# A running sum in PSUM for the seven products of Winograd's form

## The chip, the core and the metric

The kernel runs on one core of a Trainium2 chip. The metric is device time: microseconds (us) from the start of the program to its end on that core. The engines are named as the profile names them: PE multiplies matrices (PEld is its loading of weights), DVE does element-wise work on tensors, ACT does activation functions, casts and copies, POOL does further element-wise work, SP issues transfers. Each engine takes its own instructions in order; semaphores tell one engine that another is done. PE writes its sums into PSUM, a memory of eight banks; a product of 128 x 512 f32 fills one bank.

## What is computed

One layer of a backbone over 1024 latent tokens of width 1024, with a context of 256 tokens. Two token mixers (retention and mLSTM) are lifted to full width, gated and added, and a SwiGLU feed-forward follows. What the change touches are two of its projections:

```python
def mixer_output(ret, ml, rg, mo, bg_ret, bg_ml, w_ret_up, w_ml_up, w_out):
    ...
    merged = jax.nn.sigmoid(bg_ret) * (y_ret @ w_ret_up) + jax.nn.sigmoid(bg_ml) * (y_ml @ w_ml_up)
    return merged @ w_out

def swiglu(h, w_ffn_in, w_ffn_out):
    gate, up = jnp.split(h @ w_ffn_in, 2, axis=-1)
    return (jax.nn.silu(gate) * up) @ w_ffn_out
```

`bg_ret` and `bg_ml` are two groups of columns of one input projection, 1024 inputs to 1024 outputs each; `w_ffn_in` has 1024 inputs and 2 x 2816 outputs.

## The kernel before

**Precision.** Every operand is kept as two f32r parts, hi + lo. `split` (L173, L174) makes them: ACT casts the value to hi, DVE subtracts hi from it to give lo. A product is three matmuls: hi with hi, hi with lo, lo with hi.

**Blocks.** The two projections above are done in blocks of 256 outputs by 1024 inputs by 1024 tokens. Cut into halves in each dimension, a block is a 2 x 2 by 2 x 2 product of matrices, and Winograd's form of Strassen's method does it with seven products in place of eight. `seven` loads the four raw tiles of a block's weights (`raw_quads`, tiles `raw`, four buffers) and yields the seven left factors: four of them sums and differences that DVE makes (L209, tiles `stg`, three buffers), s1 to s4, and the raw a11, a12, a22. `w_pairs` splits them in the order in which they are yielded, two to a buffer (tiles `whi` and `wlo`, four buffers each). The right factors b11 to b22 and t1 to t4 are made once for all blocks of a stage.

`prod` (L228 to L231) is one product of 512 inputs, 128 outputs and 512 tokens: four steps of three matmuls each, 12 matmuls of 128 x 512 into one bank. A block is 84 matmuls.

`winograd_block` before takes seven PSUM banks, one for each product, in the order a11, a12, s2, s3, s1, s4, a22. ACT copies the first product to SBUF (L267, p1). Everything else is added by DVE, which reads a bank and a tile in SBUF (L255): u2 = second factor's product + p1, u3, u4, and the four results (0,0), (1,1), (0,1), (1,0) = (half of the outputs, half of the tokens). `ps` is one of two pools of four banks each, `mm` and `sc`; blocks take the one and the other in turn (L931, L1056), and a bank is taken again when its reader is done. The sums go to tiles `cp`, the results to tiles `sg` or `hid`, of four buffers each.

**The two stages.** In the gate stage (L908 to L931) seven blocks are done, the first of branch 1, then branch 0 and branch 1 in turn. For each of a block's four results `bg_done` follows: ACT's Sigmoid (L920), POOL's product with the lifted branch (L921), and for branch 1 DVE's sum with the result of branch 0 (L925) and a store. The first of those blocks has its partners from earlier; its tags are `hid`, those of branch 0 are `sg`. The output projection (L93 to L95) comes next and begins with the merged tiles. In the first FFN projection (L1045 to L1056) there are 20 blocks, gate and up in turn: ACT's Silu for the one (`gate_done`, L991, tiles `sg`), POOL's product and a store for the other (`up_done`, L995, L996, tiles `hid`). While a block is computed the next one's weights are loaded, added and split by `seven`.

**What sets the order.** Nothing is placed by hand: a tile scheduler puts each engine's instructions in a fixed order when the program is built, and tiles come free when their last reader is done. So the order in which ACT, DVE and PE do things around a block follows from the code's order and from the scheduler.

Of the kernel before, what the change touches and what calls it, by code (L numbers as in the profile page):

```python
# [15 lines left out]
ALU = mybir.AluOpType  # L16

P = 128
D = 1024
# [5 lines left out]
EPS = 1e-6  # L25
# [11 lines left out]
def body(tc, a, out):  # L37
# [33 lines left out]

    # ---------------------------------------------------------------- weights
    def load_w_half(src, kn, cn, hf):
# [11 lines left out]
    def load_w(src, kn, cn):  # L85
        """Loads the two halves of a block and splits each into f32r parts hi + lo."""
        return [load_w_half(src, kn, cn, hf) for hf in range(2)]

    def mm3(ps, pairs):
        """ps = sum over pairs ((lhi, llo), (rhi, rlo)) of (lhi + llo)^T (rhi + rlo)."""  # L90
        n = len(pairs)
        for i, ((lh, ll), (rh, rl)) in enumerate(pairs):
            nc.tensor.matmul(ps, lhsT=lh, rhs=rh, start=i == 0, stop=False)  # L93
            nc.tensor.matmul(ps, lhsT=lh, rhs=rl, start=False, stop=False)  # L94
            nc.tensor.matmul(ps, lhsT=ll, rhs=rh, start=False, stop=i == n - 1)  # L95

    # -------------------------------------------------------------- constants
    cpack = const.tile([P, 218], F32, name="cpack")
# [16 lines left out]
    def rsqrt_small(v, y, t):  # L115
        """y = v ** -0.5 by an integer seed and Newton steps."""
        nc.vector.tensor_scalar(out=t.bitcast(I32), in0=v.bitcast(I32), scalar1=1, scalar2=None,
                                op0=ALU.logical_shift_right)
        nc.vector.tensor_scalar(out=y.bitcast(I32), in0=t.bitcast(I32), scalar1=-1.0,
                                scalar2=float(0x5F3759DF), op0=ALU.mult, op1=ALU.add)  # L120
        for _ in range(3):
            nc.vector.tensor_tensor(out=t, in0=y, in1=y, op=ALU.mult)
            nc.vector.scalar_tensor_tensor(out=t, in0=t, scalar=-0.5, in1=v, op0=ALU.mult, op1=ALU.mult)
            nc.vector.scalar_tensor_tensor(out=y, in0=t, scalar=1.5, in1=y, op0=ALU.add, op1=ALU.mult)

    def rms_cols(parts, n):
        """(sum of squares / D + EPS) ** -0.5 of each token, as columns."""
        nb = n // P
        pc = sc_ps()[:, :nb]
        for b in range(nb):  # L130
            for i, x in enumerate(parts):
                nc.tensor.matmul(pc[:, b:b + 1], lhsT=x[:, b * P:(b + 1) * P], rhs=ones[:, 0:1],
                                 start=i == 0, stop=i == len(parts) - 1)
        v, y, t = (const.tile([P, 4], F32, tag="rms", bufs=6, name=nm("rms"))[:, :nb] for _ in range(3))
        nc.vector.tensor_scalar(out=v, in0=pc, scalar1=1.0 / D, scalar2=EPS, op0=ALU.mult, op1=ALU.add)
        rsqrt_small(v, y, t)
        dg = stage()[:, :n]
        nc.vector.tensor_tensor(out=dg.rearrange("p (b t) -> p b t", b=nb), in0=ident.unsqueeze(1).to_broadcast([P, nb, P]),
                                in1=y.unsqueeze(2).to_broadcast([P, nb, P]), op=ALU.mult)
        return dg  # L140

    def rms_bcast(dg):
        """PSUM: the columns as rows, on all partitions."""
        pr = sc_ps()[:, :dg.shape[1]]
        nc.tensor.matmul(pr, lhsT=ones, rhs=dg, start=True, stop=True)
        return pr
# [4 lines left out]
    def log_sigmoid(pl, o, x, shape, key):  # L151
        """o = min(x, 0) - log1p(exp(-|x|)), log1p by the series of 2 atanh(e / (2 + e))."""
        def t(s):
# [14 lines left out]

    # ------------------------------------------------------ Winograd's form
    tmps = []  # L170
# [20 lines left out]
    def w_pairs(blocks):  # L191
        """f32r parts hi + lo of the blocks, two to a buffer."""
        res = []
# [9 lines left out]
    def seven(src):  # L203
        """The seven left factors of Winograd's form, from the four blocks of 512 inputs x 128 columns."""
        r = raw_quads(src)

        def tt(x, y, op):
            o = stage()
            nc.vector.tensor_tensor(out=o, in0=x, in1=y, op=op)  # L209
            return o  # L210

        def gen():
            s1 = tt(r["a21"], r["a22"], ALU.add)
            yield r["a11"]
            s2 = tt(s1, r["a11"], ALU.subtract)
            yield r["a12"]
            yield s2
            yield tt(r["a11"], r["a21"], ALU.subtract)
            yield s1
            yield tt(r["a12"], s2, ALU.subtract)  # L220
            yield r["a22"]

        return w_pairs(gen())

    def prod(ps, w, x, start, stop):
        """ps (+)= w^T x over 512 inputs."""
        for k in range(4):
            c = slice(k * P, (k + 1) * P)  # L228
            nc.tensor.matmul(ps, lhsT=w[0][:, c], rhs=x[0][:, k, :], start=start and k == 0, stop=False)  # L229
            nc.tensor.matmul(ps, lhsT=w[0][:, c], rhs=x[1][:, k, :], start=False, stop=False)  # L230
            nc.tensor.matmul(ps, lhsT=w[1][:, c], rhs=x[0][:, k, :], start=False, stop=stop and k == 3)  # L231

# [16 lines left out]
    def winograd_block(ps, w, x, t, done, tag):  # L249
        a11, a12, s2, s3, s1, s4, a22 = w  # L250
        b11, b21, b12, b22 = x
        t1, t2, t3, t4 = t

        def add(p, v, o):
            nc.vector.tensor_tensor(out=o, in0=p, in1=v, op=ALU.add)  # L255
            return o

        def put(f, hf, p, v):
            done(f, hf, add(p, v, tmp(tag)))

        def product(w_, x_):
            p = ps()
            prod(p, w_, x_, True, True)
            return p

        p1, u2, u3, u4 = (tmp("cp") for _ in range(4))
        nc.scalar.copy(p1, product(a11, b11))  # L267
        put(0, 0, product(a12, b21), p1)
        add(product(s2, t2), p1, u2)
        add(product(s3, t3), u2, u3)  # L270
        p5 = product(s1, t1)
        add(p5, u2, u4)
        put(1, 1, p5, u3)
        put(0, 1, product(s4, b22), u4)
        put(1, 0, product(a22, t4), u3)

    # ------------------------------------------------- modulation and first norm
    es_ctx = ExitStack()
# [69 lines left out]
    def first_tiles(kts):  # L348
        """The first projection's products with feature tiles kts, for the first four chunks of latents."""
        for n in (2, 3, 4, 5):  # L350
# [9 lines left out]
    def tok(n, kt):  # L360
        """f32r parts of the modulated tokens of chunk n, feature tile kt."""
        if n < 2:
# [118 lines left out]
    def scan(u):  # L481
        """The two directions of a head, as stages at slots: a generator that emits a slot at a time."""
        k, v, q, g = bufs[u]
# [218 lines left out]
    def ada2():  # L702
        """Modulation columns 16 ..: two tiles of 128 at a time."""
        for cb in range(16):
# [101 lines left out]

    # ------------------------------------------------------- lift and merge
    def up_mm(br, w, y, c, dt_, hf):
# [50 lines left out]
    def diff(o, x, k, y):  # L859
        """o = x - y of feature tile k, x as f32r parts and y whole or as parts."""  # L860
        hi, lo = (v[:, k, :].bitcast(F32) for v in x)
# [79 lines left out]

    # -------------------------------------------- output projection, second norm
    x1_d = dram.tile([2, KT, P, 512], F32, name="x1_d")
# [36 lines left out]

    # --------------------------------------------------------------------- ffn
    pe = pool(es, "pe", side="right")
# [15 lines left out]
    def right_factors(k):  # L998
        """Feature tiles k of the sums and differences of the token blocks; the last stays in xf."""
        x12, x22 = xf[1][:, k, :], xf[1][:, 4 + k, :]  # L1000
# [56 lines left out]

    # ------------------------------------------------- ffn output, final norm
    es_pt.close()
# [11 lines left out]
    def w2_tiles(dp, extra=None):  # L1071
        """Weights of 256 outputs for hidden tiles 0 .. 21, as f32r parts, in order of the tiles."""
        for b in range(11):
# [14 lines left out]
    def hidden(hf):  # L1088
        """Loads and splits the hidden tiles of a half of the tokens, one at a time in order."""
        big = None  # L1090
# [112 lines left out]
def _layout(x, c, ctx, c_ctx, w_ada, b_ada, norm1_gain, norm2_gain, w_in, mlstm_gate_bias, ret_decay_logit,  # L1203
# [4 lines left out]
    def kblock(w):  # L1208
        """[K, C] -> [2, 128, K / 256, C] with row k = (2 half, K / 256, 128)."""
        k, n = w.shape  # L1210
        return w.reshape(2, k // 256, P, n).transpose(0, 2, 1, 3)
# [57 lines left out]
```

## Time and profile before

| | |
|---|---|
| median of three runs | 1644.67 us |
| lowest and highest run | 1643.19 and 1646.52 us |
| profiled execution, span of the core | 1643.1 us |
| instructions | 25962 |
| PE busy | 1604.8 us, 98% of the span |
| DVE, ACT, POOL busy | 1005.4, 631.2, 423.6 us |

The profile gives one execution's span and no other time of it; the three runs are others. Busy time is read as time in which an engine ran at least one instruction. A line such as `731.45 0.19 PEld L231 ... [0.54 <-DVE wlo L174]` of a timeline is an instruction's start in the span, its duration, engine, line, operation, what it writes and reads, and in brackets how long the engine was idle before it and whose result ended that.

### The profile page before, as it was taken

The page shows a single profiled execution, that of the slowest core. Times are in us where ns is not written, and L with a number is a line of the kernel's source. Part 1 is how long each engine was busy: PE and PEld are TensorE (multiplying, and loading weights), DVE is VectorE, ACT ScalarE, POOL GpSimd, SP SyncE. Part 2 cuts the span into 40 slices and gives each one's busy share as a digit, 9 for nine tenths or more (in the row PEclk, how much of TensorE's full clock was granted, in tenths as well). Part 3 has the DMA queues.
Part 4 walks back from the last instruction along what each step waited for, and adds up shares of the span by engine and source line. Part 5 has one row for each costly group of instructions (what it writes and reads, how often), then busy time and mean ns, then how long its engine had stood idle before and what let it go on. Part 6 is the DMA issues. An engine that isn't in the chain of part 4 may idle for free.

```text
span 1643.1 us, 25962 instructions
## 1 busy us (share of the span) xinstructions
PE 1604.8 (98%) x9326; PEld 1395.8 (85%) x9326; DVE 1005.4 (61%) x2223; ACT 631.2 (38%) x1512; POOL 423.6 (26%) x593
## 2 busy tenths in 40 slices
PE   7998999999999999999999999999999999999997
PEld 2798999999999998888877777888888888887887
DVE  5768555644645445678875777667677666536233
ACT  4555332333435355443343453323333334423230
POOL 1546244332322422233330225111111111001001
PEclk9999999999999999999999999999999999999998
DMA  9211223332432244444457412222222224735531
GB/s 328 103 62 35 73 84 104 100 101 91 136 104 91 71 149 135 161 173 161 142 183 252 130 56 71 90 96 85 96 84 83 92 88 168 268 108 179 162 103 52
DMA packets 114033, 199.13 MB, mean 121 GB/s; under 512 B 13104, under 2 KB 24048, under 8 KB 113904
## 3 DMA queue, kind: packets, MB, share of 16 engines
q1 hardware_dynamic: 112032, 195.38, 36.1%
q10 hardware_dynamic: 1872, 2.10, 0.4%
q8 instruction: 73, 1.20, 0.3%
q14 instruction: 56, 0.46, 0.1%
HBM read 160.66 MB, written 36.77 MB: 120 GB/s over the span
## 4 chain that ended last, share of the span: by engine, by line
PE 79%; DVE 7%; POOL 5%; issue 5%; DMA 2%; ACT 1%; SPq 0%; DVEq 0%; POOLq 0%; ACTq 0%
PE mm L95 9%; PE mm L93 9%; PE mm L94 9%; PE mm L1127 5%; PE mm L1129 5%; PE sc L229 5%; PE sc L230 5%; PE sc L231 5%; PE mm L1128 5%; PE mm L229 5%; PE mm L231 5%; PE mm L230 5%; PE sc L511 2%; PE sc L328 1%; POOL hid L995 1%
## 5 line engine op out<-in xcount | busy, mean ns | idle before, releaser
L93 PE MATMUL mm<-whi,A 128*128 128x256 f32 (+1 forms) x992 | 289.8, 292 | 0.9 <-DVE gtok L468 0.9
L95 PE MATMUL mm<-whi,A 128*128 128x256 f32 (+1 forms) x992 | 281.7, 284 | 0.2 <-DVE A L316 0.2
L94 PE MATMUL mm<-wlo,A 128*128 128x256 f32 (+1 forms) x992 | 281.3, 284 | 0.0
L174 DVE TENSOR_TENSOR wlo<-raw,whi 128x512 fp32r<-128x512 f32 x178 | 132.1, 762 | 114.8 <-ACT whi L173 114.6
L93 PEld LDWEIGHTS mm<-whi,A 128*128 128x128 f32 x992 | 190.3, 192 | 1.4 <-DVE gtok L468 1.1
L173 ACT CAST whi<-raw 128x512 fp32r<-128x512 f32 x178 | 106.2, 619 | 221.6 <-PE mm L1128 79.8
L95 PEld LDWEIGHTS mm<-whi,A 128*128 128x128 f32 x992 | 190.2, 192 | 0.5 <-DVE A L316 0.4
L94 PEld LDWEIGHTS mm<-wlo,A 128*128 128x128 f32 x992 | 190.6, 192 | 0.0
L995 POOL TENSOR_TENSOR hid<-hid,sg 128x512 f32<-128x512 f32 x44 | 84.8, 1931 | 329.0 <-DVE hid L255 294.0
L229 PE MATMUL mm<-A,whi 128*128 128x512 f32 x320 | 124.7, 390 | 2.4 <-DVE sg L255 1.7
L230 PE MATMUL mm<-A,whi 128*128 128x512 f32 x320 | 125.2, 391 | 1.0 <-DVE A L316 1.0
L231 PE MATMUL mm<-A,wlo 128*128 128x512 f32 x320 | 125.0, 391 | 0.0
L82 DVE TENSOR_TENSOR wlo<-raw,whi 128x512 fp32r<-128x512 f32 (+1 forms) x112 | 76.4, 708 | 53.6 <-ACT whi L81 53.6
L173 ACT CAST whi<-stg 128x512 fp32r<-128x512 f32 x108 | 61.9, 618 | 106.7 <-PE sc L230 62.2
L81 ACT CAST whi<-raw 128x512 fp32r<-128x512 f32 (+1 forms) x112 | 65.3, 619 | 41.1 <-PE mm L94 13.9
L497 POOL TENSOR_SCALAR vs<-v,colq 128x129 f32<-128x129 f32 x72 | 48.0, 676 | 127.6 <-PE sc L511 127.6
L229 PE MATMUL sc<-A,whi 128*128 128x512 f32 x208 | 80.9, 389 | 0.0
L230 PE MATMUL sc<-A,whi 128*128 128x512 f32 x208 | 80.9, 389 | 0.0
L231 PE MATMUL sc<-A,wlo 128*128 128x512 f32 x208 | 80.9, 389 | 0.0
L174 DVE TENSOR_TENSOR wlo<-stg,whi 128x512 fp32r<-128x512 f32 x108 | 80.0, 779 | 0.7 <-ACT whi L173 0.7
L1127 PE MATMUL mm<-A,whi 128*128 128x512 f32 (+1 forms) x204 | 77.8, 382 | 0.0
L1129 PE MATMUL mm<-A,wlo 128*128 128x512 f32 (+1 forms) x204 | 77.8, 381 | 0.0
(350 smaller groups left out, 4057.1 us busy)
## 6 DMA issues: line engine op xcount, KB each, us to landing
raw<-wffn SPq DMA_DIRECT2D x88, 256.0 KB
raw<-wfo SPq DMA_DIRECT2D x88, 256.0 KB
raw<-wada SPq DMA_DIRECT2D x64, 256.0 KB
raw<-win SPq DMA_DIRECT2D x60, 256.0 KB
hid_d<-hid SPq DMA_DIRECT2D x44, 256.0 KB
hraw<-hid_d SPq DMA_DIRECT2D x40, 256.0 KB
araw<-wada SPq DMA_DIRECT2D x32, 256.0 KB
bc<-rows_d SPq DMA_DIRECT2D x64, 128.0 KB
```

Of the source, the lines that this page charges most:

```text
L93: nc.tensor.matmul(ps, lhsT=lh, rhs=rh, start=i == 0, stop=False)
L94: nc.tensor.matmul(ps, lhsT=lh, rhs=rl, start=False, stop=False)
L95: nc.tensor.matmul(ps, lhsT=ll, rhs=rh, start=False, stop=i == n - 1)
L173: nc.scalar.copy(hi, x)
L174: nc.vector.tensor_tensor(out=lo, in0=x, in1=hi.bitcast(F32), op=ALU.subtract)
L229: nc.tensor.matmul(ps, lhsT=w[0][:, c], rhs=x[0][:, k, :], start=start and k == 0, stop=False)
L230: nc.tensor.matmul(ps, lhsT=w[0][:, c], rhs=x[1][:, k, :], start=False, stop=False)
L231: nc.tensor.matmul(ps, lhsT=w[1][:, c], rhs=x[0][:, k, :], start=False, stop=stop and k == 3)
L995: nc.gpsimd.tensor_tensor(out=c, in0=c, in1=sgs[f, hf], op=ALU.mult)
L1127: nc.tensor.matmul(ps, lhsT=w[0][:, c], rhs=h[0][:, t], start=kt == 0, stop=False)
L1128: nc.tensor.matmul(ps, lhsT=w[0][:, c], rhs=h[1][:, t], start=False, stop=False)
L1129: nc.tensor.matmul(ps, lhsT=w[1][:, c], rhs=h[0][:, t], start=False, stop=kt == 2 * NG - 1)
```

## The change

The seven left factors come in another order: a11, s1, s2, a12, s3, s4, a22. A block takes three banks in place of seven. In the first, `chain`, four products are added up one after the other: a11 b11, then s2 t2, s3 t3 and a22 t4, without clearing the bank between. After each of the first three ACT copies the sum so far to a tile `cp`; these are p1, u2 and u3 of before, and after the fourth ACT copies the bank as the result (1,0). The second bank takes a12 b21, and DVE adds p1 to give (0,0). The third takes s1 t1; DVE adds u3 to give (1,1); then s4 b22 is added to the same bank, and DVE adds u2 to give (0,1). So a block has three additions of DVE for seven, and four copies of ACT for one. The three matmuls a step stand in one line now (L230), and those of the added products carry the stop flag each.

```diff
         def gen():
+            yield r["a11"]
             s1 = tt(r["a21"], r["a22"], ALU.add)
-            yield r["a11"]
+            yield s1
             s2 = tt(s1, r["a11"], ALU.subtract)
+            yield s2
             yield r["a12"]
-            yield s2
             yield tt(r["a11"], r["a21"], ALU.subtract)
-            yield s1
             yield tt(r["a12"], s2, ALU.subtract)
             yield r["a22"]
...
-    def prod(ps, w, x, start, stop):
-        """ps (+)= w^T x over 512 inputs."""
+    def prod(ps, w, x, start, stop, cont=False):
         for k in range(4):
             c = slice(k * P, (k + 1) * P)
-            nc.tensor.matmul(ps, lhsT=w[0][:, c], rhs=x[0][:, k, :], start=start and k == 0, stop=False)
-            nc.tensor.matmul(ps, lhsT=w[0][:, c], rhs=x[1][:, k, :], start=False, stop=False)
-            nc.tensor.matmul(ps, lhsT=w[1][:, c], rhs=x[0][:, k, :], start=False, stop=stop and k == 3)
+            for i, (wp_, xp) in enumerate(((0, 0), (0, 1), (1, 0))):
+                nc.tensor.matmul(ps, lhsT=w[wp_][:, c], rhs=x[xp][:, k, :], start=start and k == i == 0,
+                                 stop=cont or (stop and k == 3 and i == 2), skip_group_check=cont)
...
     def winograd_block(ps, w, x, t, done, tag):
-        a11, a12, s2, s3, s1, s4, a22 = w
+        a11, s1, s2, a12, s3, s4, a22 = w
         b11, b21, b12, b22 = x
         t1, t2, t3, t4 = t
-        def add(p, v, o):
-            nc.vector.tensor_tensor(out=o, in0=p, in1=v, op=ALU.add)
+        def put(f, hf, p, v):
+            c = tmp(tag)
+            if v is None:
+                nc.scalar.copy(c, p)
+            else:
+                nc.vector.tensor_tensor(out=c, in0=p, in1=v, op=ALU.add)
+            done(f, hf, c)
+
+        def snap(p):
+            o = tmp("cp")
+            nc.scalar.copy(o, p)
             return o
-        def put(f, hf, p, v):
-            done(f, hf, add(p, v, tmp(tag)))
-
-        def product(w_, x_):
-            p = ps()
-            prod(p, w_, x_, True, True)
-            return p
-
-        p1, u2, u3, u4 = (tmp("cp") for _ in range(4))
-        nc.scalar.copy(p1, product(a11, b11))
-        put(0, 0, product(a12, b21), p1)
-        add(product(s2, t2), p1, u2)
-        add(product(s3, t3), u2, u3)
-        p5 = product(s1, t1)
-        add(p5, u2, u4)
-        put(1, 1, p5, u3)
-        put(0, 1, product(s4, b22), u4)
-        put(1, 0, product(a22, t4), u3)
+        chain, second, third = ps(), ps(), ps()
+        prod(chain, a11, b11, True, True)
+        p1 = snap(chain)
+        prod(third, s1, t1, True, True)
+        prod(chain, s2, t2, False, True, True)
+        u2 = snap(chain)
+        prod(second, a12, b21, True, True)
+        put(0, 0, second, p1)
+        prod(chain, s3, t3, False, True, True)
+        put(1, 1, third, snap(chain))
+        prod(third, s4, b22, False, True, True)
+        put(0, 1, third, u2)
+        prod(chain, a22, t4, False, True, True)
+        put(1, 0, chain, None)
```

The rest of the diff takes out comments. Outside the two stages the engines' orders are as before.

**PE between s3 and s4.** The rows below are PE's order at one place in an ordinary FFN block, where the product of s3 (`whi_12240`, `wlo_12241`) ends. A name is a tile with its number: `mm_` and `sc_` are banks, `t_` and `A_` right factors, `whi_` and `wlo_` the parts of left factors; `mm_12399` is `chain` and `mm_12401` `third`. Before, at the same row numbers:

```order
L229 MATMUL mm_12515<-t_11729,whi_12288 128x512
L230 MATMUL mm_12515<-t_11730,whi_12288 128x512
L231 MATMUL mm_12515<-t_11729,wlo_12289 128x512
L229 MATMUL mm_12532<-A_11691,whi_12288 128x512
L230 MATMUL mm_12532<-A_11692,whi_12288 128x512
L231 MATMUL mm_12532<-A_11691,wlo_12289 128x512
```

After:

```order
L230 MATMUL mm_12399<-t_11691,whi_12240 128x512
L230 MATMUL mm_12399<-t_11692,whi_12240 128x512
L230 MATMUL mm_12399<-t_11691,wlo_12241 128x512
L230 MATMUL sc_12542<-A_11264,whi_12369 128x512
L230 MATMUL sc_12542<-A_11265,whi_12369 128x512
L230 MATMUL sc_12542<-A_11264,wlo_12370 128x512
L230 MATMUL sc_12542<-A_11264,whi_12369 128x512
L230 MATMUL mm_12399<-A_11649,whi_12248 128x512
L230 MATMUL mm_12399<-A_11650,whi_12248 128x512
L230 MATMUL mm_12399<-A_11649,wlo_12249 128x512
L230 MATMUL mm_12401<-A_11649,whi_12240 128x512
L230 MATMUL mm_12401<-A_11650,whi_12240 128x512
```

Before, each product goes to a bank of its own and the next follows at once. Now the scheduler puts seven matmuls between the products of s3 and s4: four of the next block's a11 (bank `sc_12542`) and three of a22 (back into `chain`).

**ACT in the first FFN block.** These are ACT's instructions from the copy of the block's first sum on, with the semaphores that each waits for (`DMAHW` is a transfer, `Activation` ACT itself). Before:

```order
L267 COPY cp_12151<-mm_12155 128x512 [waits PE_49]
L173 CAST whi_12123<-raw_12113 128x512 [waits DMAHW7_49,PE_49]
L173 CAST whi_12123<-raw_12119 128x512 [waits DMAHW3_49]
L991 ACTIVATE sg_12182<-sg_12182 128x512 [waits DVE_49]
L173 CAST whi_12131<-stg_12127 128x512 [waits PE_49,Activation_49]
```

After, with `mm_12109` as `chain`:

```order
L266 COPY cp_12124<-mm_12109 128x512 [waits PE_49]
L173 CAST whi_12079<-raw_12071 128x512 [waits DMAHW7_49,PE_49]
L173 CAST whi_12079<-stg_12083 128x512 [waits DVE_49]
L266 COPY cp_12150<-mm_12109 128x512 [waits PE_49]
L173 CAST whi_12089<-stg_12087 128x512 [waits DVE_49,PE_49,Activation_49]
L173 CAST whi_12089<-raw_12077 128x512 [waits DMAHW3_49]
L998 ACTIVATE sg_12164<-sg_12164 128x512 [waits DVE_49]
L266 COPY cp_12179<-mm_12109 128x512 [waits PE_49,Activation_49]
```

The second copy of `chain` (`cp_12150`) now stands behind the casts of the next block's a11 (a raw tile) and s1 (a sum that DVE makes), the third (`cp_12179`) behind those of s2 and a12 and a Silu.

**ACT in the first gate block**, from the second copy of `chain` (`mm_9813`) to the third, after:

```order
L266 COPY cp_9854<-mm_9813 128x512 [waits PE_49]
L173 CAST whi_9775<-raw_9767 128x512 [waits DMAHW4_49,Activation_49]
L927 ACTIVATE hid_9868<-hid_9868 128x512 [waits DVE_49]
L173 CAST whi_9785<-raw_9773 128x512 [waits DMAHW7_49,PE_49,Activation_49]
L173 CAST whi_9775<-stg_9779 128x512 [waits DVE_49]
L173 CAST whi_9785<-stg_9783 128x512 [waits DVE_49]
L266 COPY cp_9886<-mm_9813 128x512 [waits PE_49]
```

Between the two copies stand four casts of the next block's factors and a Sigmoid; before, ACT had no copy here.

## Rows read from the trace of the kernel before

**Rows 1.** The page's first part: busy time by engine, whole span.

```profile
PE 1604.8 (98%) x9326; PEld 1395.8 (85%) x9326; DVE 1005.4 (61%) x2223; ACT 631.2 (38%) x1512; POOL 423.6 (26%) x593
```

**Rows 2.** Stretches: from:to, length, PE PEld DVE ACT POOL busy, clock, DMA, GB/s.

```profile
722.50:858.00 135.50, 135.38 (x597) 111.73 (x596) 107.53 (x150) 55.83 (x98) 45.15 (x31) 1.00 0.54 177
1001.00:1024.00 23.00, 21.30 (x95) 17.30 (x94) 11.75 (x20) 6.78 (x12) 8.29 (x4) 1.00 0.39 126
1024.00:1384.00 360.00, 360.00 (x1590) 298.10 (x1589) 247.19 (x345) 115.06 (x196) 60.34 (x39) 1.00 0.27 91
```

**Rows 3.** PE's waits from 640 to 1400: in total, times, longest.

```profile
PE mm L229 <- DVE sg L255: 1.7, 1, 1.7
```

**Rows 4.** Timeline of the first gate block, PE, PEld, DVE, ACT.

```profile
722.51 0.40 PE L229 MATMUL mm<-A,whi 128*128 128x512 f32 x1
...
725.22 0.69 DVE L209 TENSOR_TENSOR stg<-stg,raw 128x512 f32<-128x512 f32 x1 [0.79 <-DMA up_d<-stg]
...
731.45 0.19 PEld L231 LDWEIGHTS mm<-t,wlo 128*128 128x128 f32 x1 [0.54 <-DVE wlo L174]
...
736.54 0.62 ACT L173 CAST whi<-raw 128x512 fp32r<-128x512 f32 x1 [1.34 <-DMA raw<-wbg]
...
737.90 1.78 DVE L174 TENSOR_TENSOR wlo<-raw,whi 128x512 fp32r<-128x512 f32 x1
```

**Rows 5.** Timeline of the end of the gate stage, PE and DVE.

```profile
856.05 0.39 PE L231 MATMUL mm<-A,wlo 128*128 128x512 f32 x1
...
859.50 0.68 DVE L255 TENSOR_TENSOR hid<-mm,cp 128x512 f32<-128x512 f32 x1
```

**Rows 6.** Instructions of L255: ns min/median/max, first and last start.

```profile
L255 DVE TENSOR_TENSOR cp<-sc,cp x39: 676/691/693, 755.4 to 1378.7; 128x512 f32<-128x512 f32 x39
```

**Rows 7.** Timeline of the first FFN block, ACT and DVE.

```profile
1004.07 0.59 ACT L267 COPY cp<-mm 128x512 f32<-128x512 f32 x1 [1.03 <-PE mm L231]
...
1013.93 0.69 DVE L209 TENSOR_TENSOR stg<-raw,raw 128x512 f32<-128x512 f32 x1 [9.54 <-DMA raw<-wffn]
```

**Rows 8.** Groups of the scans' matmuls: count | busy, mean ns | idle.

```profile
L511 PE MATMUL sc<-vs,k 128*128 128x129 f32 x144 | 24.4, 276 | 0.0
...
L571 PE MATMUL sc<-sb,qs 128*128 128x128 f32 x64 | 12.4, 275 | 0.0
```

**Rows 9.** Timeline of an FFN block: a first product's end and its copy.

```profile
1100.83 0.39 PE L231 MATMUL sc<-A,wlo 128*128 128x512 f32 x1
...
1101.32 0.59 ACT L267 COPY cp<-sc 128x512 f32<-128x512 f32 x1 [1.17 <-PE sc L231]
```

**Rows 10.** Timeline of a branch-1 gate block: ACT, DVE and POOL.

```profile
770.00 0.62 ACT L173 CAST whi<-raw 128x512 fp32r<-128x512 f32 x1 [1.61 <-DMA raw<-wbg]
...
770.53 0.63 ACT L920 ACTIVATE hid<-hid 128x512 f32<-128x512 f32 x1
...
770.65 0.69 DVE L174 TENSOR_TENSOR wlo<-raw,whi 128x512 fp32r<-128x512 f32 x1 [1.01 <-ACT whi L173]
...
771.23 1.29 POOL L921 TENSOR_TENSOR hid<-hid,pr 128x512 f32<-128x512 f32 x1 [2.14 <-ACT hid L920]
```

**Rows 11.** Timeline: PE's wait in the first FFN block.

```profile
1015.87 0.68 DVE L255 TENSOR_TENSOR sg<-mm,cp 128x512 f32<-128x512 f32 x1
...
1016.61 0.50 PE L229 MATMUL mm<-A,whi 128*128 128x512 f32 x1 [1.70 <-DVE sg L255]
...
1016.95 0.40 PE L230 MATMUL mm<-A,whi 128*128 128x512 f32 x1
```

**Rows 12.** Timeline: PE in the output projection, behind the gate stage.

```profile
864.37 0.73 PE L93 MATMUL mm<-A,whi 128*128 128x512 f32 x2 [3.18 <-ACT A L173]
...
866.64 0.63 PE L93 MATMUL mm<-A,whi 128*128 128x512 f32 x1
867.07 0.63 PE L94 MATMUL mm<-A,whi 128*128 128x512 f32 x1
```

**Rows 13.** The stretch of those matmuls, columns as in rows 2.

```profile
866.60:869.20 2.60, 2.60 (x7) 1.98 (x6) 2.60 (x5) 0.00 (x0) 0.00 (x0) 0.50 0.88 295
```

## The prediction

> **What bounds the kernel now.** I read the page first: PE is busy for 1604.8 us of a span of 1643.1 us, 98% [rows 1]. Two stages hold the 27 blocks that the change touches: 7 in the gate stage (722.5 to 858) and 20 in the first FFN projection (1001 to 1384). The busy times by stage show PE idle for 0.1 us of 135.5 in the one, for 1.7 of 23 and then for nothing of 360 in the other, its clock at full (1.00), and room on DVE and ACT everywhere [rows 2]. The list of PE's waits has one behind the blocks' additions, of 1.7 us [rows 3]. So a block lasts as long as its 84 matmuls. From the first start at 722.51 [rows 4] to the last at 856.05 [rows 5] lie 587 spacings of 0.227 us: 2.73 a product, 19.1 a block. Removed DVE work can give back little; what counts is each new wait of PE.
>
> **What goes and comes.** Four of seven additions leave DVE: 27 x 4 x 0.69 = 75 us of 1005 [rows 1, 6]. Three copies a block come to ACT: 27 x 3 x 0.59 = 48 us on top of 631 [rows 1, 7]. Both lie beside PE; by themselves they cost and give nothing. The matmuls are as many, on the same operands; in the added products each carries the stop flag, which I price at nothing: a scan's matmuls that start and stop at once (L511) take 276 ns, those that do neither (L571) 275 [rows 8]. Bounds 0 and 1 ns.
>
> **The new waits in an ordinary block.** Four products now add into one bank, and PE may go on in it only when ACT's copy is done. Two of those copies have another product (2.73 us) as cover. The third does not: it ends in the addition for (1,1), which reads the bank that s4 then adds to. The order puts seven matmuls in between: four of the next block, three of a22.
> From rows: a copy starts 0.49 us after the start of the product's last matmul (1100.83 to 1101.32) [rows 9] and takes 0.59; DVE follows 0.03 after ACT (770.62 to 770.65) [rows 10] and adds in 0.69 [rows 6]; PE follows 0.06 after DVE (1016.55 to 1016.61), and a matmul that had to wait is followed by the next 0.34 later, not 0.23 [rows 11]. PE follows 0.05 after ACT (864.32 to 864.37; ACT's cast is 0.62) [rows 12]. So a wait costs release minus slot plus 0.11.
> Counted from the start of s3's last matmul: copy 0.49 to 1.08, PE released at 1.13; the slot of a22 is the fifth, 1.135, so near that I count the 0.11. Addition 1.11 to 1.80, PE released at 1.86; the slot of s4 is 1.135 + 0.11 + 0.68 = 1.92: hardly a wait, 0.04 as half a chance of the 0.11 with its rest. Together 0.15, if ACT and DVE are free when called. They should be: the casts before the copy start with the end of the product of a12, 2.7 us earlier, and two casts with a Silu behind them fill 0.53 + 0.62 + 0.63 us. Bounds: 0 if the cover is a little longer, 0.75 if one instruction is still running ahead of the copy or the addition. I take 0.15, the worked row. In 22 blocks (19 FFN, 3 gate): **+3.3** (0 to 16.5).
> PE's wait for a reader of its bank is in the trace: at 1016.61 it starts 0.06 us after the DVE addition that read the bank [rows 11]. The Trainium skill (PSUM — Partial Sum Buffer, "PSUM bank collisions raise a hardware error") says that two engines must not be in one bank at once, a rule against a running sum that is copied out between products; the trace agrees. Could PE add while ACT copies, the 0.11 of a22 would go, and this term fall to 0.9.
>
> **Second-branch gate blocks.** Here DVE's last addition for (0,0), which needs ACT's Sigmoid and a POOL product, now stands ahead of the addition for (1,1). Counted as above, (0,0) is added and two casts are made from -2.24 (the end of a12's product) on; casts 0.53 + 0.62, Sigmoid 0.63, POOL 1.29 [rows 10], DVE 0.60 to its next: (1,1) would start at 1.5, PE be released at 2.3, 0.35 behind the slot, 0.46 with the 0.11. With the 0.11 of a22 0.56, or 0.75 if POOL takes 0.2 longer; two blocks: **+1.3** (0.3 to 1.9).
>
> **First gate block.** It starts at 722.51 with weights that are still being made. s1 is now second. Its cast and low part stand behind DVE's difference, which ends at 725.91 [rows 4]: ready 726.57 against a slot of 725.69 (by the order 14 spacings on); cost 1.0 with the 0.11. ACT has three casts of the next block ahead of the third copy, the first of them at 736.54, when its raw tile has landed [rows 4]; the two behind it need DVE's sums and end at 738.8. Copy 738.8 to 739.4 against a slot at 738.03: 1.5. DVE has seven instructions ahead of the addition for (1,1), 0.6 each from 736.6 on, one of them 1.78 long beside POOL as at 737.90 [rows 4]: it starts at 742.6 and gives PE 743.4 against 742.5, although the order has 17 matmuls there: 1.0. The stall at 731.45 [rows 4] goes; its slot was 38 spacings on, 731.14, so 0.4 is won. **+3.1** (0.6 to 4.5).
>
> **First FFN block.** Its successor's weights land late: DVE idles 9.5 us until 1013.93 [rows 7]. Before, that reached PE only through a bank, at 1016.61: the 60th spacing from 1001.08 gives 1014.70, so the loss was 1.91 + 0.11 = 2.0 [rows 11]. Now ACT's copy after s2 stands behind the cast of the next block's s1, which needs that sum: 1013.93 + 0.69, cast to 1015.27, copy to 1015.8, PE released at 1015.85. The slot of s3: the first copy's start, 1004.07 [rows 7], less 0.49 and eleven spacings is the block's start, 1001.08; four products more give 1011.98. Cost 4.0. With the ordinary 0.15, net **+2.1** (0.2 to 2.2). The stall cannot be hidden: the transfer's place in SP's queue behind stores stays.
> PE would idle there for some 3.8 us. An idle of 3.18 that ends at 864.37 is followed by matmuls 0.43 apart (866.64, 867.07) [rows 12], at a granted clock of 0.50, the 1.2 GHz level [rows 13]; the waits at 731.45 and 1016.61 (0.54 and 1.70) left it at 1.00 over their stretches [rows 2]. Nearest to 3.18: some eight matmuls 0.2 late, **+1.6** (0 to 1.6).
>
> **End of the gate stage.** (1,0) is now copied by ACT. Its bank was ready at 856.05 + 0.49, but DVE came to it at 859.50, behind a POOL result [rows 5]; then PE idles 3.18 us for its split [rows 12]. In the new order ACT's copy waits its turn behind the Sigmoid of (0,1), whose addition waits for POOL likewise. I walk the chain to within a microsecond of the old one, and a small stall of s4 there hides in the idle: **0** (-0.9 to +0.7).
>
> **Sum.** 3.3 + 1.3 + 3.1 + 2.1 + 1.6 = 11.4 us on the profiled span of 1643.1: 1654.5. The median of the runs, 1644.67, lies 1.6 above the span, so 1656.1. All low ends give 0.2 more than before, all high ends 27: 1645 to 1672.
>
> **Rivals.**
> The cover holds: s4 and a22 never wait, raw tiles land a little earlier. Then some 2 us of the first gate block stays, 1646.7. For it: the ordinary slots miss by a tenth only. Against: the two first blocks do not hang on it. 0.17.
> Not slower, but faster: the end of the gate stage. If ACT copies (1,0) as soon as a22 is done, 3.0 us earlier than DVE did (856.5 for 859.50), the idle of 3.18 all but goes and the half clock behind it too: 3.0 + 1.6 less small costs of about 1, 1641. It decides when the copy stands ahead of (0,1)'s Sigmoid; the order has it behind. 0.08.
> ACT or DVE is late in every block: one more cast or low part in front of the copy or the addition, 0.6 in each of 22 blocks, 13 on top of the rest: some 1669. For it: in-order queues whose casts wait for transfers. Against: in the ordinary block I count nearly a microsecond of slack on ACT. 0.12.
> The clock falls at each of the 27 small gaps: 27 x 1.6 = 43, some 1695. Against: the wait of 1.70 at 1016.61 left the clock at 1.00 [rows 2, 11]. 0.03. The Trainium skill (TensorE: Matmul & The Clock Gate, "A second HAM failure mode: psum-queue depth-cycling") tells of a kernel whose short idles at bank changes made the clock swing; by it this rival would be the forecast, and the trace does not bear it out.
>
> **Numbers.** Forecast 0.60. A measurement of this kernel tells about 0.2% (3.3 us) from no change. Faster by more: 0.07, from the second rival. Within: 0.18, the first rival and a rest. Slower by more: 0.75. The range leaves out the clock rival, the faster case and half of the late-queue case: 1646 to 1668.
>
> **What would show it.** In the profile after: PE waits at L230 for DVE's addition and for ACT's copies, some 27 of each, of 0.3 us at most in ordinary FFN blocks; one wait of some 3.8 us about 1012 to 1016 for a copy; DVE's busy time down by 75 us, ACT's up by 48. If PE's waits in ordinary blocks are over half a microsecond, the term of the cover is wrong; if the wait near 1012 is missing, the cast did not stand in the way; if the stretch from 1024 on lasts as long as before and the gate stage too, the first rival has won. What makes it wrong above all is a tenth of a microsecond in the cover, taken 22 times.

## The result and the profile after

Four runs of the changed kernel have a median of 1656.57 us (1651.68 to 1657.73), beside 1644.91 us before. The ratio is 1.0065, with a 95% interval of 1.0047 to 1.0083: slower by 11.7 us. The forecast was 1656.1. The profiled execution has a span of 1655.2 us, 12.1 more than that of before; the forecast of the span was 1654.5.

The page's first part, to be held beside [rows 1]:

```profile
PE 1613.2 (97%) x9326; PEld 1394.2 (84%) x9326; DVE 947.2 (57%) x2115; ACT 674.7 (41%) x1593; POOL 421.1 (25%) x593
```

PE has the same 9326 matmuls. DVE has 108 instructions fewer (27 x 4) and ACT 81 more (27 x 3). ACT's busy time rose by 43.5 us and DVE's fell by 58.2, less than the 75 counted: the additions that went take 72 us by their rows, DVE's other instructions took some 5 us more, and where rows overlap busy time counts once.

PE's waits in the gate stage (722 to 862), and behind it the one of the FFN blocks (990 to 1400), as total, times and longest; to be held beside [rows 3]:

```profile
PE mm L230 <- DVE hid L261: 1.2, 2, 0.7
PE mm L230 <- DVE wlo L174: 0.7, 1, 0.7
PE mm L230 <- ACT cp L266: 0.7, 1, 0.7
PE mm L230 <- ACT whi L173: 0.3, 1, 0.3
```

```profile
PE mm L230 <- ACT cp L266: 2.8, 1, 2.8
```

All but the wait on `whi` and `wlo` (s1 is not ready in the first gate block) are waits for a reader of a shared bank: L266 is ACT's copy of `chain`, L261 DVE's addition out of `third`. The 1.7 us of [rows 3] is gone, 2.8 us stands in its place.

**An ordinary FFN block**, in the timeline (start, duration, engine, line, operation), from the last matmul of s3 on; PEld's rows show the short waits in brackets:

```profile
1101.46 0.39 PE L230 MATMUL mm<-t,wlo 128*128 128x512 f32 x1
...
1101.94 0.58 ACT L266 COPY cp<-mm 128x512 f32<-128x512 f32 x1 [1.28 <-PE mm L230]
...
1102.58 0.30 PEld L230 LDWEIGHTS mm<-A,whi 128*128 128x128 f32 x2 [0.25 <-ACT cp L266]
1102.59 0.73 PE L230 MATMUL mm<-A,whi 128*128 128x512 f32 x2
1102.62 0.69 DVE L261 TENSOR_TENSOR sg<-mm,cp 128x512 f32<-128x512 f32 x1 [1.50 <-ACT cp L266]
...
1103.37 0.30 PEld L230 LDWEIGHTS mm<-A,whi 128*128 128x128 f32 x2 [0.26 <-DVE sg L261]
1103.39 0.71 PE L230 MATMUL mm<-A,whi 128*128 128x512 f32 x2
```

The copy starts 0.48 us after the start of s3's last matmul and takes 0.58. PE's row at 1102.59 joins the first two matmuls of a22. The first starts 0.23 us after its predecessor, as always, but its weight load (PEld) has waited for the copy, and the second follows 0.33 us later and not 0.23. The row at 1103.39 joins the first two of s4, 0.32 apart, behind the wait of the weight load for the addition out of `third`. Each hold costs a tenth of a microsecond. From 1030 to 1385 PEld has 18 such waits for the copy and 18 for the addition, where before it had none:

```profile
PEld mm L230 <- DVE sg L261: 2.3, 9, 0.3
PEld mm L230 <- ACT cp L266: 2.2, 9, 0.2
PEld sc L230 <- ACT cp L266: 1.7, 9, 0.2
PEld sc L230 <- DVE hid L261: 1.7, 9, 0.2
```

In what follows two traces are set side by side by matmul: both have 9326, and the start of each is compared with the start of the one that has the same place in PE's order before. So compared, the delay grows over the 19 ordinary FFN blocks from 8.31 us to 11.60: 0.173 us a block, 0.22 where the block is in the pool `mm` and 0.13 where it is in `sc`.

**The first FFN block**: ACT's copy behind the cast of the next block's s1, PE's wait for it, and the matmuls after it.

```profile
1018.47 0.69 DVE L209 TENSOR_TENSOR stg<-raw,raw 128x512 f32<-128x512 f32 x1 [8.73 <-DMA raw<-wffn]
```

```profile
1019.20 0.62 ACT L173 CAST whi<-stg 128x512 fp32r<-128x512 f32 x1 [2.12 <-DVE stg L209]
1019.72 0.58 ACT L266 COPY cp<-mm 128x512 f32<-128x512 f32 x1
```

```profile
1020.35 0.73 PE L230 MATMUL mm<-t,whi 128*128 128x512 f32 x2 [2.80 <-ACT cp L266]
1020.92 0.39 PE L230 MATMUL mm<-t,wlo 128*128 128x512 f32 x1
1021.15 0.89 PE L230 MATMUL mm<-t,whi 128*128 128x512 f32 x2
1021.84 0.63 PE L230 MATMUL mm<-t,wlo 128*128 128x512 f32 x1
```

The chain is the forecast's: weights land, DVE adds (1018.47), ACT casts (1019.20), only then copies, and PE goes on at 1020.35. The matmuls from 1021.84 on last 0.63 in place of 0.39; that stretch (columns as in [rows 2]) has the granted clock of 0.50, the 1.2 GHz level:

```profile
1021.84:1024.40 2.56, 2.56 (x7) 1.98 (x6) 2.38 (x4) 0.63 (x1) 0.00 (x0) 0.50 0.47 179
```

### The profile page after: what moved, and what is told of

Same layout as the page of the kernel before. It is cut to its first block, busy times and chain, and to the rows that moved or that the text cites. A ratio compares the mean times of both kernels' runs of the same rounds, so it can differ in the third digit from the quotient of the medians.

```text
span 1655.2 us, 25920 instructions
## 1 busy us (share of the span) xinstructions
PE 1613.2 (97%) x9326; PEld 1394.2 (84%) x9326; DVE 947.2 (57%) x2115; ACT 674.7 (41%) x1593; POOL 421.1 (25%) x593
## 4 chain that ended last, share of the span: by engine, by line
PE 75%; issue 8%; DVE 7%; POOL 6%; DMA 2%; ACT 2%; SPq 0%; POOLq 0%; DVEq 0%; ACTq 0%
PE mm L230 12%; PE sc L230 12%; PE mm L95 9%; PE mm L93 9%; PE mm L94 9%; PE mm L1134 5%; PE mm L1136 5%; PE mm L1135 5%; PE sc L518 2%; PE sc L335 1%; POOL hid L928 1%; POOL hid L1002 1%; POOL sg L928 1%; POOL xf L322 1%; POOL stg L322 1%
## 5 line engine op out<-in xcount | busy, mean ns | idle before, releaser
L174 DVE TENSOR_TENSOR wlo<-raw,whi 128x512 fp32r<-128x512 f32 x178 | 139.7, 800 | 148.0 <-ACT whi L173 142.0
L230 PE MATMUL mm<-A,whi 128*128 128x512 f32 x640 | 203.8, 396 | 3.9 <-DVE hid L261 1.2
L230 PEld LDWEIGHTS mm<-A,whi 128*128 128x128 f32 x640 | 117.9, 188 | 36.9 <-ACT cp L266 4.3
L230 PE MATMUL sc<-A,whi 128*128 128x512 f32 x416 | 131.5, 392 | 0.0
L230 PE MATMUL mm<-A,wlo 128*128 128x512 f32 x320 | 125.2, 392 | 0.0
L230 PE MATMUL mm<-t,whi 128*128 128x512 f32 x336 | 104.9, 394 | 3.1 <-ACT cp L266 2.8
L230 PE MATMUL sc<-t,whi 128*128 128x512 f32 x312 | 96.1, 389 | 0.0
L230 PEld LDWEIGHTS sc<-A,whi 128*128 128x128 f32 x416 | 76.3, 188 | 19.5 <-ACT cp L266 2.5
L174 DVE TENSOR_TENSOR wlo<-stg,whi 128x512 fp32r<-128x512 f32 x108 | 83.5, 794 | 0.2
L230 PE MATMUL sc<-A,wlo 128*128 128x512 f32 x208 | 81.4, 391 | 0.0
```

The lines of the kernel that those rows point to most:

```text
L174: nc.vector.tensor_tensor(out=lo, in0=x, in1=hi.bitcast(F32), op=ALU.subtract)
L230: nc.tensor.matmul(ps, lhsT=w[wp_][:, c], rhs=x[xp][:, k, :], start=start and k == i == 0, stop=cont or (stop and k == 3 and i == 2), skip ...
```

## The experiments

**A fourth bank.** s4 leaves the bank that the addition for (1,1) reads; the running sum stays.

```diff
...
-        put(1, 1, third, snap(chain))
-        prod(third, s4, b22, False, True, True)
-        put(0, 1, third, u2)
+        u4 = tmp("cp")
+        nc.vector.tensor_tensor(out=u4, in0=third, in1=u2, op=ALU.add)
+        put(1, 1, third, snap(chain))
+        prod(fourth, s4, b22, True, True)
+        put(0, 1, fourth, u4)
```

> The changed kernel, but the product of s4 goes to a fourth bank and DVE adds u2 to the third one first (four additions a block in place of three). In the order s4's 12 matmuls now stand between s3 and a22, so both short covers are gone and everything else stays. Theory (PE waits for the readers of a shared bank, each wait is release minus slot): the 0.18 us of each of 19 FFN blocks goes (3.4), 0.3 in the gate's ordinary blocks, 0.4 in each of two second-branch blocks, and in the first gate block both waits of 0.93 and 0.96; together some 6 us, 1650 to 1651. The wait of some 3 us in the first FFN block stays, since the running sum stays. Rival (the price is in the copies or in the stop flags, not in the cover): 1656 to 1657 as before the edit.

Measured: 1649.47 us (1.0026 of before, 1.0015 to 1.0037), 7.1 less than the changed kernel. In the trace every ordinary block is back at 19.04 us; in the same 320 us of FFN blocks PE does 1413 matmuls, against 1401 in the changed kernel (columns as in [rows 2], first this kernel, then the changed one):

```profile
1050.00:1370.00 320.00, 320.00 (x1413) 265.06 (x1412) 190.82 (x256) 129.16 (x226) 48.42 (x32) 1.00 0.28 87
```

```profile
1050.00:1370.00 320.00, 320.00 (x1401) 260.42 (x1400) 180.80 (x239) 126.90 (x221) 51.59 (x34) 1.00 0.27 87
```

ACT has its copies still (129 us busy) and three products of each block carry the stop flag; so neither costs PE anything. In the ordinary blocks the short covers are the whole cost. In the gate stage PE has no wait for a copy or an addition left, and in this execution s1 was ready, which the expectation did not count on (the time is 0.5 us under its range). What stays is the wait in the first FFN block, 3.5 us in this execution:

```profile
PE mm L230 <- ACT cp L266: 3.5, 1, 3.5
```

**A bank for each product.** Factor order, additions and copies are those of the change; the sums from one product to the next are left out, and in PE's order s4 follows s3 at once.

```diff
...
-        prod(chain, s2, t2, False, True, True)
+        chain = ps()
+        prod(chain, s2, t2, True, True)
...
-        prod(chain, s3, t3, False, True, True)
+        chain = ps()
+        prod(chain, s3, t3, True, True)
...
-        prod(third, s4, b22, False, True, True)
+        third = ps()
+        prod(third, s4, b22, True, True)
...
-        prod(chain, a22, t4, False, True, True)
+        chain = ps()
+        prod(chain, a22, t4, True, True)
```

> The changed kernel with its factor order, its three additions and its four copies, but each product in a bank of its own: the sums from one product to the next are left out, so the values are not the layer's. Theory (sharing a bank is what costs; copies and fewer additions cost and give nothing by themselves): all waits at L230 for copies go, the one in the first FFN block too, and with it the half clock; only the first gate block's s1 that is not ready stays (1.5 us): 1643 to 1647. Rival (ACT's three copies a block push its casts late): no less than 1653.

Measured: 1644.13 us (0.9995, 0.9986 to 1.0004), the time of before. PE's waits in the gate stage up to 862 and in the FFN blocks:

```profile
PE mm L230 <- DVE wlo L174: 0.7, 1, 0.7
PE mm L95 <- DVE wlo L82: 0.5, 1, 0.5
```

```profile
PE mm L230 <- ACT cp L266: 0.7, 1, 0.7
```

The same work on ACT and DVE, with no bank shared, costs nothing beyond s1's low part in the first gate block (0.9 us, matmul by matmul). The late weights still hold ACT's copy back, but PE meets that only when a bank comes round again: 0.7 us in place of 2.8, and of 1.7 before. So the first FFN block gives 0.9 back, and the equal time is in part that balance. Two things follow: the sharing of banks is the cause, and 75 us of DVE instructions taken away are worth nothing here.

**The first FFN block as before.** One block of 27 keeps the old form and factor order.

```diff
...
-        winograd_block((mm_ps, sc_ps)[i % 2], cur, b_all, t_all, done, tag)
+        (old_block if i == 0 else winograd_block)((mm_ps, sc_ps)[i % 2], cur, b_all, t_all, done, tag)
```

> The changed kernel with the first of the 20 FFN blocks in the form and factor order of before. Theory (there the second copy of the running sum waits on ACT behind the cast of a sum whose weights land late, and the idle drops the clock): the wait of 2.8 us and the half clock behind it (1.6) go, the old wait of 1.7 us comes back: 2.5 to 2.8 us less, 1654. Rival (the weights are late for the next block anyway, whoever waits): 1656 to 1657.

Measured: 1653.13 us (1.0050, 1.0037 to 1.0063), 3.4 less than the changed kernel where 2.5 to 2.8 was expected. The waits from 1000 to 1050 (line numbers have moved):

```profile
PE mm L241 <- DVE sg L266: 1.5, 1, 1.5
PE sc L241 <- ACT cp L305: 1.5, 1, 1.5
```

The old wait came back, as expected, and the half clock was gone. But a second wait stands in the block behind, the first in the new form (1.8 us lost): the weights' delay reaches the next running sum. Matmul by matmul the two blocks together lost 1.7 us, 1.4 less than in the changed kernel, so the gain at this place is about half of the expected one; the rest of the 3.4 lies where the two kernels are the same (the gate stage began 1.8 us earlier in this execution). The block that shares a bank pays, whichever it is. So the first block's form is not the cause but the place where it shows; the next experiment goes to the transfer itself.

**The weights early.** The four raw tiles of the second FFN block are issued by ACT and not behind SP's stores. In the changed kernel SP's queue reads (three stores that wait for POOL's results, then the loads):

```profile
1010.91 2.81 SPq L1003 DMA_DIRECT2D hid_d<-hid  x3
1013.84 1.37 SPq L188 DMA_DIRECT2D raw<-wffn  x3
```

```diff
...
-            nxt = seven(a["wffn"][blocks[i + 1]])
+            nxt = seven(a["wffn"][blocks[i + 1]], nc.scalar if i == 0 else None)
```

> The changed kernel with one thing moved: the four raw weight tiles of the second of the 20 FFN blocks are issued on ACT's queue and not on SP's, where they stood behind three stores. Nothing else in the engines' orders changes. Theory (in the first FFN block ACT's copy of the running sum waits behind the cast of a sum whose weights come late, and the idle halves the clock for a while): the wait of 2.8 us shrinks to half a us or goes, the half clock (1.6) goes: 4 to 4.7 us less than the changed kernel, 1652 to 1652.6. Rival (the wait is ACT's own order, not the transfer): 1656 to 1657.

Measured: 1651.94 us (1.0036, 1.0022 to 1.0051), 4.6 less than the changed kernel. ACT issues the first load at 1002.77; SP came to it at 1013.84, which is 1011.6 by this execution's clock, in which PE reached the block 2.2 us earlier. The cast of the sum is over 1.8 us before the second copy of `chain` is due:

```profile
1002.77 0.34 ACTq L188 DMA_DIRECT2D raw<-wffn  x1
...
1007.36 0.59 ACT L266 COPY cp<-mm 128x512 f32<-128x512 f32 x1 [1.98 <-PE mm L230]
...
1010.24 0.61 ACT L173 CAST whi<-stg 128x512 fp32r<-128x512 f32 x1
1012.65 0.59 ACT L266 COPY cp<-mm 128x512 f32<-128x512 f32 x1 [1.80 <-PE mm L230]
```

The list of PE's waits in the FFN blocks is empty, the half clock gone, and the 2.0 us that before lost at that place [rows 11] too. At this place the gain is 4.8 us, matmul by matmul. ACT's order is the same in both, so the transfer's place in SP's queue is what makes this wait; ACT's order and the shared bank are the way in which it reaches PE. Whether another order on ACT would do as well was not run.

**One more addition.** A double of the addition for (1,1) is put ahead of it.

```diff
-        put(1, 1, third, snap(chain))
+        u3 = snap(chain)
+        o = tmp("cp")
+        nc.vector.tensor_tensor(out=o, in0=third, in1=u3, op=ALU.add)
+        put(1, 1, third, u3)
```

> The changed kernel with one more addition of DVE in each block, a double of the one for (1,1), put right ahead of it (its result is not used), so that the third bank comes free 0.6 us later. The order answers: ten matmuls stand between s3 and s4 in place of seven (six of a22 for three), 0.68 us more. Theory (the cost is release minus slot, and the filler pays for it): ordinary blocks cost 0.1 to 0.2 us as before, 1655 to 1658 in all. Rival (a bank's reader costs PE its own time, whatever stands between): 0.6 in each of 27 blocks, some 1672.

Measured: 1653.83 us (1.0053, 1.0035 to 1.0072). The same 320 us of FFN blocks hold 1404 matmuls, three more than in the changed kernel:

```profile
1050.00:1370.00 320.00, 320.00 (x1404) 261.85 (x1403) 188.61 (x254) 125.55 (x220) 49.89 (x32) 1.00 0.27 87
```

A bank held 0.6 us longer cost nothing, since the scheduler put three more matmuls (0.68 us) in between; the blocks even lost 0.12 each in place of 0.17, and PEld's waits for the addition are gone from its list while those for the copy stay. A shared bank costs what its cover lacks, and not what its reader takes. The total came out 1.2 us below the range that was expected; its first gate block lost 1.7 in place of 3.0, since s1's low part was late by 0.2 there and not 0.7.

**The gate stage alone.** The FFN blocks have the old form.

```diff
...
-    nxt = seven(a["wffn"][1, 0])
+    nxt = seven(a["wffn"][1, 0], True)
...
-        winograd_block((mm_ps, sc_ps)[i % 2], cur, b_all, t_all, done, tag)
+        old_block((mm_ps, sc_ps)[i % 2], cur, b_all, t_all, done, tag)
```

> The running sum in the seven gate blocks alone; the FFN blocks have the form and factor order of before. Theory (each stage's loss is its own): the gate stage loses 4.3 us as in the trace of the changed kernel (3.0 in the first block, 0.9 in the two second-branch blocks, 0.4 in the others), the FFN nothing: 1649.3. Rival (the gate stage's loss is hidden by the idle at its end): 1645 to 1646.

Measured: 1648.51 us (1.0016, 1.0007 to 1.0025), 2.7 more than before in the same session. Matmul by matmul the gate stage lost 3.8 us in the profiled execution, and the FFN blocks gained 0.8, as their first block's wait came out at 0.9 and not 1.7. So the gate stage's loss is not hidden by the idle at its end. That the total is 0.8 us below the expected one has its counterpart in that gain: how late the weights land differs from one execution to the next.

**Another way to the idle behind the gate stage.** In the kernel before, the product of a22 is moved ahead of s1 and s4.

```diff
+            yield r["a22"]
             yield s1
             yield tt(r["a12"], s2, ALU.subtract)
-            yield r["a22"]
...
-        a11, a12, s2, s3, s1, s4, a22 = w
+        a11, a12, s2, s3, a22, s1, s4 = w
...
+        put(1, 0, product(a22, t4), u3)
         p5 = product(s1, t1)
         add(p5, u2, u4)
         put(1, 1, p5, u3)
         put(0, 1, product(s4, b22), u4)
-        put(1, 0, product(a22, t4), u3)
```

> The kernel before, seven banks, with one thing moved: the product of a22 stands ahead of s1 and s4, so that the result (1,0), which the output projection's first half needs, is done two products (5.4 us) earlier. If the idle of 3.18 us behind the gate stage is the time of that result's chain (Sigmoid, POOL, addition, split), it goes, with the half clock behind it (1.6): some 4.5 to 5 us less than before, 1640. If the idle is set by something else (the slots of the right factors, the weights of the projection), 1645. (1,1) is later then, but is needed only in the projection's second half, 20 us on.

Measured: 1640.84 us (0.9974, 0.9964 to 0.9983). Of PE's waits between 722 and 1000 the 3.18 us at [rows 12] is gone, and the half clock with it; matmul by matmul 5.57 us are gained there. These waits are left:

```profile
PE mm L230 <- DVE A L316: 0.9, 3, 0.3
PE mm L231 <- DVE wlo L174: 0.9, 1, 0.9
PE mm L95 <- DVE wlo L82: 0.7, 1, 0.7
PE mm L229 <- ACT A L314: 0.7, 1, 0.7
```

**Both moves together**: a22 early, and the four loads on ACT's queue.

```diff
...
-            nxt = seven(a["wffn"][blocks[i + 1]])
+            nxt = seven(a["wffn"][blocks[i + 1]], nc.scalar if i == 0 else None)
```

> The kernel before with a22 ahead of s1 and s4, and the same move of the four transfers to ACT's queue. In the run with a22 early alone PE waited 1.1 us at 1010 for an addition behind sums whose weights came late; that wait should go: 1.2 to 1.3 us less than 1640.8, some 1639.5. Rival (the transfers are slowed by the stores they now run beside, or they push ACT's casts): 1640.8 or more.

Measured: 1638.22 us (0.9960, 0.9946 to 0.9975), faster than both kernels. Between 990 and 1400 PE waits for nothing; the place of [rows 11] gains 1.99 us against before, where a22 early alone gained 0.57. So the second move is worth 1.4 us there, near the 1.2 to 1.3 expected; that the time fell by 2.6 has its rest at other places, which differ between executions (the first gate block lost 0.1 for 0.9).

## Why the prediction held, step by step

The terms, in us, as put and as measured, matmul by matmul, between the two profiled executions:

| term | put | measured |
|---|---|---|
| first gate block | 3.1 | 3.0 |
| second-branch gate blocks | 1.3 | 0.9 |
| ordinary blocks, 3 gate and 19 FFN | 3.3 | 3.7 |
| first FFN block | 2.1 | 1.4 |
| half clock behind it | 1.6 | 1.6 |
| end of the gate stage | 0 | -0.1 |
| ahead of the gate stage | not put | 1.1 |
| behind the FFN blocks | not put | 0.5 |
| span | 11.4 | 12.1 |

**What bounds it.** PE, and new waits alone count: the bank for each product shows it, with DVE's and ACT's work as changed and the time as before. The chance of faster by the end of the gate stage did not come: ACT's copy of (1,0) came at 865.08, behind a Sigmoid, as the order has it, and PE went on at 871.18 after 2.55 us of idle:

```profile
864.55 0.63 ACT L927 ACTIVATE hid<-hid 128x512 f32<-128x512 f32 x1 [1.31 <-DVE hid L261]
865.08 0.57 ACT L259 COPY hid<-mm 128x512 f32<-128x512 f32 x1
```

**The cover.** Right in mechanism and nearly in size. The 0.11 for a22 was 0.10 in the pool `mm`. s4's wait, which I put at 0.04 as a slot that is just missed, was 0.09 there. In `sc` both were smaller, 0.05 and 0.02; the rest of each block's loss is in steps of about 0.01 over the matmuls behind them. The fourth bank shows that these two waits are all of it.

What the sum had only roughly is where a wait begins to cost. It is PE's weight load that waits, and it otherwise starts a spacing ahead of its matmul (at 1102.14 for the matmul at 1102.36). In `mm` blocks a22's load starts 0.02 us ahead of its matmul's slot, and 0.10 is lost; in `sc` blocks, where the copy comes 0.05 sooner after s3's last matmul (why, no trace shows), it starts 0.07 ahead, and 0.05 is lost; s4's load there starts 0.09 ahead, and 0.02 is lost. With one more addition s4's load starts 0.19 ahead of the later slot, and nothing is lost. So a release that only just makes the slot is already late; by these rows it has to come some 0.2 us before it. The `sc` rows:

```profile
1082.72 0.59 ACT L266 COPY cp<-sc 128x512 f32<-128x512 f32 x1 [1.80 <-PE sc L230]
...
1083.36 0.30 PEld L230 LDWEIGHTS sc<-A,whi 128*128 128x128 f32 x2 [0.19 <-ACT cp L266]
1083.42 0.67 PE L230 MATMUL sc<-A,whi 128*128 128x512 f32 x2
```

What the prediction calls a rule against a running sum that is copied out between products is here a price and no bar: ACT's copies and PE's matmuls take turns in `chain`, and a turn costs the hold.

**Second-branch blocks.** The wait for (1,1) behind (0,0) came in both, 0.26 over a spacing and 0.11 after it; 0.47 a block, not 0.65. (1,1)'s addition started 1.45 us after s3's last matmul where 1.5 was put and let PE go at 2.2 for 2.3, and a22 lost 0.04 and not 0.11: the slow end that I had averaged in was not needed, though POOL's product did take 0.2 longer.

**First gate block.** The sum was right by parts that were not. s1 cost 1.5 for 1.0: its cast was late too, not only its low part. The third copy cost 0.9 for 1.5, the addition for (1,1) 0.96 for 1.0, the old stall gave 0.4 back. How much of it an execution shows hangs on when the weights land: with one more addition the block lost 1.7, with the gate stage alone changed 2.8, with the first FFN block as before 3.6.

**First FFN block.** The mechanism was right to the instruction, the size too large: the wait with its 0.11 behind it cost 3.07 for 4.0 (the table's 1.4 holds the block's own two short holds too, as the term put does, and is less the 2.0 that before lost there). The step that was mis-sized is the time of the weights' arrival, taken as fixed from one execution: counted from the block's start DVE's sum came 0.8 earlier than before. In the run with a fourth bank the same wait was 3.5.

**What was not put.** The stage began 1.1 us later than in the profile of before, where nothing had changed; over the ten profiles here its start lies between 0.85 us earlier and 1.13 later. Behind the FFN blocks 0.5 was lost; the other executions lie between 0.3 less and 2.0 more than before there, and the kernel with both moves, which shares no bank, at 1.3 more. So 1.6 of the 12.1 us are play between executions, and the match to within a microsecond is in part luck: terms too small by 0.4 and too large by 1.3, and 1.6 that no term had. One of the four runs of the changed kernel took 1651.68; what was different in it no trace shows.

**The clock.** The rival in which every small gap lowers the clock is out: 19 blocks with two gaps each kept a granted clock of 1.00. (Its price was also added up short: 1644.7, the 9.8 of the other terms and 43 are 1698 and not 1695.) The Trainium skill (TensorE: Matmul & The Clock Gate, "A second HAM failure mode: psum-queue depth-cycling") tells of short idles at bank changes that made the clock swing; for gaps of a tenth of a microsecond, as here, it is no forecast.

## What to carry to other kernels

Where PE is the bound, as here, an addition that moves from DVE into PSUM saved nothing, and each copy of a running sum is a hold on the bank: count copy, then addition, then release, against the matmuls that the order puts in between, to a tenth of a microsecond, and give a product that would follow such a reader too closely a bank of its own if one is free. A reader of a bank that stands on an in-order engine inherits that engine's worst wait; look there for a cast or a sum whose data is still being loaded, and at the queue that issues the load. Read an idle of the bounding engine back to the result that it waits for, and ask whether that result could be computed earlier: here that made the kernel 4.2 us faster, and the change made it 11.7 slower.

## What was not expected of the hardware

An idle of PE of about 3 us does not always halve the clock. Behind the gate stage it was 3.18 us before, 2.55 in the changed kernel, both with six or seven matmuls 0.43 apart after it; in the run with early weights 2.56 us at the same place left the clock at full, and so did 2.84 us there in the run with one more addition. The stretch behind the idle, first in the changed kernel and then in the one with early weights (columns as in [rows 2], the third column from the end is the clock):

```profile
871.80:874.30 2.50, 2.50 (x7) 1.96 (x6) 2.50 (x5) 1.87 (x4) 0.00 (x0) 0.50 0.68 184
```

```profile
870.30:873.00 2.70, 2.68 (x11) 1.94 (x12) 2.70 (x5) 2.15 (x4) 0.00 (x0) 1.00 0.74 225
```

And a shorter one can: in the run with a22 early 1.01 us of idle at 1502.74, with eight matmuls of one column behind it, was followed by eight at the half clock (0.43 apart, 1503.65 on; the granted clock from 1503.85 to 1507.20 is 0.50). What decides it the runs do not show; the term of 1.6 us was right because it happened, and could have been 0.

```profile
1502.74 1.05 PE L132 MATMUL sc<-ones,hid 128*128 128x1 f32 x8 [1.01 <-DVE hid L1177]
1503.65 0.62 PE L1128 MATMUL mm<-h,whi 128*128 128x512 f32 x1
1504.07 0.63 PE L1129 MATMUL mm<-h,wlo 128*128 128x512 f32 x1
```
